# A two-layer decoder trunk: head groups of the attention in turns, sample taps of the convolution as one product and a sum, the first norm reordered

## The chip, the cores and the metric

The kernel runs on one core of a Trainium2 chip. The metric is the device time of one execution in microseconds, median of three runs. Names of engines as the profile has them: PE is TensorE (matrix products, PEld its loads of weights), DVE is VectorE, ACT is ScalarE, POOL is GpSimd, SP is SyncE, which here only issues DMAs.

## The reference, cut to what matters

One step of a two-layer decoder runs over 512 positions of a prompt and 64 of samples (8 samples of 8 positions), which share all weights: 576 columns. Each layer is a half feed-forward step, a mixer, and another half feed-forward step, each behind an RMS norm. The mixer has three branches: a causal depthwise convolution of width 31, a gated spatial product (gMLP), and attention over a sliding window of 128 positions with 8 query heads in 2 kv groups.

```python
x = x + 0.5 * swiglu(rms_norm(x, n1), gu1, dn1)
z = rms_norm(x, nm) @ w_in      # GLU | gMLP u,v | q | k | v | three gates
xp = concat([conv_prev, a])     # per sample: 30 old rows, 8 new ones
c = depthwise_conv(xp, w_conv_dw) + b_conv_dw              # 31 taps
y_a = silu(layer_norm(c)) @ w_conv_out
y_b = (u * (w_s @ layer_norm(v) + b_s)) @ w_gmlp_out
s = einsum('qkgd,skd->kgqs', q, k) * 64 ** -0.5            # per kv group k
y_c = einsum('kgqs,skd->qkgd', softmax_with_sink(s), v) @ w_o
x = x + (sig(gA)*y_a + sig(gB)*y_b + sig(gC)*y_c) @ w_out
x = x + 0.5 * swiglu(rms_norm(x, n2), gu2, dn2)
```

The prompt's attention goes by blocks of 128 queries; a block sees the key block before it and its own, the first only its own. Each sample attends to 128 cached keys and its own 8.

## The kernel before, in words

**Layout.** Activations lie with features on the 128 partitions and the 576 columns along them. Every large product of fp32 numbers is done as three products of rounded parts (high x high, high x low, low x high), each as two matmuls of 288 columns; these are the lines L327, L330 and L333 (`mm3`), a "plain" product below. The first products of a feed-forward step are combined from seven half products (`product`, L574, called from p1 to p7, and named "pair" in the list of weights), except the first three of layer 0, which are plain (`plainly`). Weights come by SP's queue into `wr` and `wc` tiles, are rounded by ACT and their low part is made by DVE, or, for some blocks of the pairs (`by_dma`), by a DMA that POOL issues and that adds in place.

**Order.** A scheduler lists the instructions of each engine by a priority: the stream of plain products advances it, `_At` shifts an engine's instruction earlier (HI, 10 million) or later (LOW). PE takes its list in order; `cpe` is PE at HI, but behind the last matmul of the stream that stands in `mark`. The mixer's small work (attention, norms, spatial products) runs as generators in `chains`: after every four input tiles of a plain product (24 matmuls, one "step") each chain is moved on by one `yield`. The numbers W_A, W_B, W_G, W_C and their like say how many steps a chain waits at a place. PSUM has two `z` tiles for the stream, two `m` tiles for norms and spatial products, and two `n` tiles, which the attention uses.

**Attention** (`attention`). After the norms and the rotation of q and k, `sample_scores` makes for each kv group 2 x (4 products of 32 columns of the array, one of 128), `sample_values` transposes the softmax and multiplies with the values. Then `scores(c, kv)` goes through 4 blocks of 2 groups one by one: four products of 256 columns in two n tiles, each read by DVE (mask added) into `sp`, then `soft`; `values(c, kv)` transposes `sp` by way of an n tile into `ptp`, and multiplies with `vT`. A kv group takes 64 rows of the array in the scores and 64 columns in the values. Two groups are in flight, and every group takes three steps.

**Convolution.** For each of four channel tiles, `tap(k)` multiplies a shifted window of `cb` with tap k and adds to `c`: one DVE instruction over the 512 prompt columns and one over the 64 sample columns, 31 times. They are put into `later` and issued in small numbers by `filler` behind products; what is left is issued ahead of the convolution's norm.

**Norms.** `square` sums the squares of x in tiles of tag g (two buffers). `rstd_steps` multiplies these sums with `ones` (L86 with `m`), takes the inverse root by Newton steps on DVE (`newton`, tiles nv, nt, no), splits the result into `oh` and spreads it over the columns by products with `idr`, the identity. `layer_norm` does the same for the gMLP and the convolution after its mean. At the start `ones` and `idr` are written after the first loads.

Of the kernel before, what the change touches and what calls it, by code (L numbers as in the profile page):

```python
# [93 lines left out]

@with_exitstack
def trunk(ctx: ExitStack, tc: tile.TileContext, a):
# [3 lines left out]
    ve, se, ge, sy = (_At(tc, e, HI) for e in (nc.vector, nc.scalar, nc.gpsimd, nc.sync))  # L100
    pe = nc.tensor
# [4 lines left out]
    lve = _At(tc, nc.vector, LOW)  # L106
# [309 lines left out]
    def square(k):  # L416
        sq = slot("g", "sq")
# [100 lines left out]
    nc.scalar.dma_start(out=vec[:, 0, 0:8], in_=a["vec"][:, 0, 0:8])  # L518
    for k in range(KD):
# [12 lines left out]
    nc.vector.tensor_copy(out=idr, in_=idn[:, 0:P])  # L532
# [4 lines left out]
    nc.vector.memset(ones, 1.0)  # L537
# [30 lines left out]
    def product(out, form, b, first):  # L568

        h, lo, n = form  # L570
        for k in range(n):
            bh, bl = b[k]
            for i, (w, r) in enumerate(((h, bh), (h, bl), (lo, bh))):
                e = pe.matmul(out=out, lhsT=w[:, k, :], rhs=r, start=first and k == 0 and i == 0,  # L574
                              stop=k == n - 1 and i == 2, skip_group_check=True)
        mark["mm"] = e.ins

    def ffn(l, f, nxt):
# [3 lines left out]
        for k0, k1 in chunks(l, f):  # L582
# [57 lines left out]
            def plainly(j):  # L640

                nonlocal r, tops
                if j == 0:
# [8 lines left out]
                    g = rstd_steps(acc["t"], 1.0 / D, EPS, r, w=1)  # L652
# [102 lines left out]
    def mixer(l, xd, nxt):  # L755
# [18 lines left out]
        def attention():  # L774
# [80 lines left out]

            def sample_scores():
                for kv in range(2):
                    zz = mtile("n")
                    r = slice(64 * kv, 64 * kv + 64)
                    for g in range(2):  # L860
                        for b in range(4):
                            cpe.matmul(out=zz[32 * b:32 * b + 32, 192 * g:192 * g + P],
                                       lhsT=qs[r, 4 * g + b].rearrange("p j t -> p (j t)"),
                                       rhs=ck[r, P * (4 * g + b):P * (4 * g + b + 1)], start=True, stop=True)
                        cpe.matmul(out=zz[:, 192 * g + P:192 * (g + 1)],
                                   lhsT=qs[r, 4 * g:4 * g + 4].rearrange("p b j t -> p (b j t)"),
                                   rhs=kk[r, TP:T], start=True, stop=True)
                    ave.scalar_tensor_tensor(out=s[:, 384 * kv:384 * (kv + 1)], in0=zz[:, 0:384], scalar=0.125,
# [4 lines left out]
            def sample_values():  # L873
# [11 lines left out]
                for kv in range(2):  # L885
                    r = slice(64 * kv, 64 * kv + 64)
                    for g in range(2):
# [3 lines left out]
                        for b in range(4):  # L891
                            bb = 4 * g + b
# [6 lines left out]
            def scores(c, kv):  # L899
# [3 lines left out]
                r = slice(64 * kv, 64 * kv + 64)  # L903
                s4 = big("sp", "sp").rearrange("p (j n) -> p j n", j=4)[:, :, 0:w]
                msk = con[:, C_MP + o0:C_MP + 256].rearrange("p (o n) -> p o n", o=1).to_broadcast([P, 2, w])
                for j in (0, 2):
                    z = mtile("n").rearrange("p (i n) -> p i n", i=2)
                    for i in range(2):
                        cpe.matmul(out=z[:, i, 0:w], lhsT=q4[r, j + i, c * P:(c + 1) * P], rhs=kk[r, k0:k0 + w], start=True, stop=True)
                    ave.scalar_tensor_tensor(out=s4[:, j:j + 2, :], in0=z[:, :, 0:w], scalar=0.125, in1=msk, op0=ALU.mult, op1=ALU.add)  # L910
                soft(s4, vcol(l, V_SP + 4 * kv, 4), lambda t: t, w, "p")
                return values(c, kv, s4, w // P, k0, r)

            def values(c, kv, s4, nk, k0, r):
                pt = big("pt", "ptp")
                for b in range(nk):
                    zt = mtile("n")
                    for j in range(4):
                        cpe.transpose(zt[:, j * P:(j + 1) * P], s4[:, j, b * P:(b + 1) * P], ident)
                    ase.activation(out=pt[:, 512 * b:512 * (b + 1)], in_=zt, func=AF.Copy)  # L920
# [9 lines left out]
            yield  # L930
            ready = [sample_values()]
            for c in range(4):
                for kv in range(2):
# [7 lines left out]
            drain(ready.pop(0))  # L941
            yield
            next(ready[0])
            yield from wait(W_B)
            drain(ready[0])
# [333 lines left out]
```

## Time and profile before

| | us |
|---|---|
| median of 3 runs (2607.34 to 2609.54) | 2608.89 |
| profiled execution | 2607.47 |
| its span in the trace | 2605.7 |
| PE busy (mean granted clock 0.995) | 2577.6 |
| DVE busy | 1910.9 |
| ACT busy | 1272.8 |
| POOL busy | 291.3 |

Busy time is that of the one profiled execution. PE's records of matmuls overlap, so that the distance from one start to the next is the cost of one, not its length. An fp32 product appears as two records: the `x8` of a group of four such products are eight records. A wait of an engine is listed with what released it; a "granted clock" of 0.5 in a stretch is the lower of TensorE's two clocks.

### The profile page before, as it was taken

How to read it: one execution, taken by the hardware profiler on the slowest of the kernel's cores; microseconds unless marked ns; L12 is line 12 of the kernel's file. 1: busy time of each engine (PE TensorE's matmuls, PEld its weight loads, DVE VectorE, ACT ScalarE, POOL GpSimd, SP SyncE). 2: the span in 40 equal slices, each digit the busy share in tenths (PEclk: the TensorE clock that was granted, in tenths of full speed). 3: DMA queues.
4: the chain of work that ended last, by engine and by line, in shares of the span. 5: the costliest groups of instructions: out<-in, count | busy, mean ns of one | idle time of the engine just before them, and what ended most of it. 6: DMA issues, size and time to landing. Idle time of an engine off the chain costs nothing.

```text
span 2605.7 us, 49108 instructions
## 1 busy us (share of the span) xinstructions
PE 2577.6 (99%) x18996; PEld 2519.0 (97%) x18996; DVE 1910.9 (73%) x3488; ACT 1272.8 (49%) x2415; POOL 291.3 (11%) x317
## 2 busy tenths in 40 slices
PE   8999999999999999999999999999999999999999
PEld 7999999988899999999999999999889999999999
DVE  7676675698897785766885766747988977766665
ACT  6455453335524564554674644533454245644543
POOL 0111010010010010111110111100200100111110
PEclk9999999999999999999999999999999999999999
DMA  5565554231222464655554655633312234655653
GB/s 179 131 147 139 125 125 132 84 87 65 66 82 81 138 150 126 147 132 132 139 129 125 146 136 132 133 116 87 85 59 68 86 96 136 145 131 143 130 143 89
DMA packets 196222, 307.48 MB, mean 118 GB/s; under 512 B 39690, under 2 KB 56970, under 8 KB 195988
## 3 DMA queue, kind: packets, MB, share of 16 engines
q1 hardware_dynamic: 159124, 237.47, 30.0%
q0 software_dynamic: 36720, 66.86, 16.0%
q8 instruction: 149, 2.44, 0.4%
q14 instruction: 85, 0.70, 0.1%
q10 hardware_dynamic: 144, 0.00, 0.0%
HBM read 292.47 MB, written 8.84 MB: 116 GB/s over the span
## 4 chain that ended last, share of the span: by engine, by line
PE 94%; DVE 3%; DMA 1%; ACT 1%; issue 1%; POOL 0%; SPq 0%; DVEq 0%; POOLq 0%; ACTq 0%
PE z L327 18%; PE z L330 17%; PE z L333 17%; PE z L574 15%; PE n L574 10%; PE m L574 10%; PE n L86 4%; PE m L86 2%; DVE w L88 1%; ACT w L88 0%; DVE x L88 0%; DMA rt<-q 0%; DMA wr<-w_gu 0%; DVE c L88 0%; DVE sums L88 0%
## 5 line engine op out<-in xcount | busy, mean ns | idle before, releaser
L88 ACT ACTIVATE w<-wr 128x512 fp32r<-128x512 f32 (+2 forms) x575 | 337.8, 604 | 625.7 <-PE z L333 487.7
L574 PE MATMUL z<-xh,w 128*128 128x288 f32 x2040 | 444.5, 299 | 1.1 <-DVE no L88 1.1
L88 ACT ACTIVATE w<-wc 128x512 fp32r<-128x512 f32 (+2 forms) x467 | 257.8, 583 | 303.2 <-PE z L333 133.1
L88 POOL DMA_DIRECT2D w<-w_gu x255 | 220.2, 864 | 1507.3 <-ACT w L88 980.7
L327 PE MATMUL z<-xh,w 128*128 128x288 f32 x1520 | 337.1, 303 | 8.0 <-ACT w L88 6.6
L88 DVE TENSOR_TENSOR w<-sums,w 128x512 fp32r<-128x512 f32 x340 | 234.4, 689 | 149.4 <-ACT w L88 145.0
L574 PEld LDWEIGHTS z<-xh,w 128*128 128x128 f32 x2040 | 338.6, 188 | 4.3 <-DVE z L88 1.3
L330 PE MATMUL z<-xl,w 128*128 128x288 f32 x1520 | 327.3, 296 | 0.0
L333 PE MATMUL z<-xh,w 128*128 128x288 f32 x1520 | 327.2, 296 | 0.0
L327 PE MATMUL z<-ah,w 128*128 128x288 f32 x1408 | 303.3, 296 | 0.4
L330 PE MATMUL z<-al,w 128*128 128x288 f32 x1408 | 301.8, 296 | 0.4 <-DVE al L88 0.2
L574 PE MATMUL z<-xl,w 128*128 128x288 f32 x1020 | 301.7, 296 | 0.0
L88 DVE TENSOR_TENSOR w<-wr,w 128x512 fp32r<-128x512 f32 (+2 forms) x373 | 240.6, 645 | 82.6 <-ACT w L88 81.6
L333 PE MATMUL z<-ah,w 128*128 128x288 f32 x1408 | 300.9, 295 | 0.0
L88 ACT ACTIVATE w<-sums 128x512 fp32r<-128x512 f32 x340 | 212.0, 624 | 139.7 <-PE z L574 73.4
L327 PEld LDWEIGHTS z<-xh,w 128*128 128x128 f32 x1520 | 245.5, 191 | 22.2 <-issue 11.7
L330 PEld LDWEIGHTS z<-xl,w 128*128 128x128 f32 x1520 | 247.5, 190 | 0.7 <-issue 0.7
L333 PEld LDWEIGHTS z<-xh,w 128*128 128x128 f32 x1520 | 246.1, 190 | 0.4 <-issue 0.3
L88 DVE SCALAR_TENSOR_TENSOR c<-cb,vec,c 128x512 f32<-128x512 f32 x480 | 244.5, 556 | 0.2
L327 PEld LDWEIGHTS z<-ah,w 128*128 128x128 f32 x1408 | 226.5, 188 | 2.5 <-DVE x L88 2.3
L330 PEld LDWEIGHTS z<-al,w 128*128 128x128 f32 x1408 | 226.5, 189 | 1.4 <-DVE al L88 1.1
L333 PEld LDWEIGHTS z<-ah,w 128*128 128x128 f32 x1408 | 226.5, 188 | 0.0
(255 smaller groups left out, 4805.0 us busy)
## 6 DMA issues: line engine op xcount, KB each, us to landing
w<-w_gu POOLq DMA_DIRECT2D x255, 256.0 KB, 4.6
wc<-w_gu SPq DMA_DIRECT2D x219, 256.0 KB, 3.0
wr<-w_in SPq DMA_DIRECT2D x184, 256.0 KB, 2.8
wr<-w_gu SPq DMA_DIRECT2D x149, 256.0 KB, 3.0
wc<-w_dn SPq DMA_DIRECT2D x75, 256.0 KB, 3.1
wr<-w_dn SPq DMA_DIRECT2D x53, 256.0 KB, 3.1
wr<-w_out SPq DMA_DIRECT2D x32, 256.0 KB, 3.2
wc<-w_dn SPq DMA_DIRECT2D x40, 128.0 KB, 2.9
```

The source lines that it names most:

```text
L86: r = f(*args, **kw)
L88: r = f(*args, **kw)
L327: pe.matmul(out=z[c], lhsT=wh, rhs=rh[:, s], start=first, stop=False)
L330: pe.matmul(out=z[c], lhsT=wh, rhs=rl[:, s], start=False, stop=False)
L333: e = pe.matmul(out=z[c], lhsT=wl, rhs=rh[:, s], start=False, stop=last)
L574: e = pe.matmul(out=out, lhsT=w[:, k, :], rhs=r, start=first and k == 0 and i == 0, stop=k == n - 1 and i == 2, skip_group_check=True)
```

## The change

1. **Attention by blocks.** `scores(c)` and `values(c)` take both kv groups, with the kv loop innermost: products of kv 0 and kv 1 stand in turns, each group with its own n tile in the scores and both in one n tile in the values, and the softmax of both is issued together. There are 4 turns of 5 steps (W_A is 4 where it was 1, W_B is 1) in place of 8 of 3. `sample_scores` and `sample_values` are turned in the same way; the `sample_scores` have their 128-column products at their end.
2. **gMLP norm.** W_G[2], the steps between the Newton steps and the products with `idr`, is 5 instead of 3.
3. **Sample taps.** The 64-column half of `tap` goes. For each channel tile four `taps(i)` are added at the end of its entries in `later` (35 instead of 31 entries): over two samples one product of an overlapping view of `cb` (2 x 8 x 31 elements, 496 columns) with the 31 taps, one sum over the last axis, and an ACT instruction that adds the bias.
4. **Start.** 22 products of `ones` with `ones` into an m tile stand ahead of the stream; `ones`, `idn` (now on ACT's DMA queue) and `idr` are written first. The squares use tag s (12 buffers), the first norm's Newton steps go to DVE and ACT at twice HI, and its sums of squares are issued ahead of the n tile's product (`next(g)`); `rms` too uses twice HI.
5. **`product`** is issued behind the last matmul in `mark`, as `cpe` is.

```diff
-W_M, W_A = 2, 1
-W_G, W_C = (4, 4, 3, 3), (2, 3, 2)
+W_M, W_A = 2, 4
+W_G, W_C = (4, 4, 5, 3), (2, 3, 2)
...
+N_WARM = 22
...
+    hve, hse = (_At(tc, e, 2 * HI) for e in (nc.vector, nc.scalar))
...
-        drain(rstd_steps(acc["t"], 1.0 / D, EPS, r))
+        drain(rstd_steps(acc["t"], 1.0 / D, EPS, r, hve, hse))
...
+    idn = slot("c", "idn")
+    nc.scalar.dma_start(out=idn[:, 0:P], in_=a["idn"])
+    hve.memset(ones, 1.0)
+    zw = mtile()
+    for i in range(N_WARM):
+        pe.matmul(out=zw[:, 0:P], lhsT=ones, rhs=ones, start=True, stop=True)
+    hve.tensor_copy(out=idr, in_=idn[:, 0:P])
...
     for k in range(KD):
-        square(k)
-    idn, selr = slot("c", "idn"), big("pt", "selr")
-    nc.sync.dma_start(out=idn[:, 0:P], in_=a["idn"])
+        square(k, "s")
...
-        for k in range(n):
+        with tc.issue_after(mark["mm"]):
+            for k in range(n):
...
-                    g = rstd_steps(acc["t"], 1.0 / D, EPS, r, w=1)
+                    g = rstd_steps(acc["t"], 1.0 / D, EPS, r, hve, hse, 1)
+                    next(g)
...
-                    for i in range(2):
-                        cpe.matmul(out=z[:, i, 0:w], lhsT=q4[r, j + i, c * P:(c + 1) * P], rhs=kk[r, k0:k0 + w], start=True, stop=True)
+                    for i in range(2):
+                        for kv, r in enumerate(KV):
+                            cpe.matmul(out=z[kv][:, i, 0:w], lhsT=q4[r, j + i, c * P:(c + 1) * P], rhs=kk[r, k0:k0 + w],
+                                       start=True, stop=True)
...
                 for b in range(nk):
-                    cpe.matmul(out=zo[r, :], lhsT=vT[:, k0 // P + b, r], rhs=pt[:, 512 * b:512 * (b + 1)],
-                               start=(b == 0), stop=(b == nk - 1))
-                ase.activation(out=q4[r, :, c * P:(c + 1) * P], in_=zo[r, :].rearrange("p (j n) -> p j n", j=4), func=AF.Copy)
+                    for kv, r in enumerate(KV):
+                        cpe.matmul(out=zo[r, :], lhsT=vT[:, k0 // P + b, r], rhs=pt[kv][:, 512 * b:512 * (b + 1)],
+                                   start=(b == 0), stop=(b == nk - 1), skip_group_check=True)
+                ase.activation(out=q4[:, :, c * P:(c + 1) * P], in_=zo.rearrange("p (j n) -> p j n", j=4), func=AF.Copy)
...
-            yield
-            ready = [sample_values()]
+            yield from wait(W_A)
+            last = sample_values()
+            next(last)
+            yield from wait(W_B)
             for c in range(4):
-                for kv in range(2):
-                    ready.append(scores(c, kv))
-                    yield from wait(W_A)
-                    if len(ready) > 2:
-                        drain(ready.pop(0))
-                    yield
-                    next(ready[-2])
-                    yield from wait(W_B)
...
+                g = scores(c)
+                yield from wait(W_A)
+                drain(last)
+                last = g
+                next(last)
+                yield from wait(W_B)
+            drain(last)
...
-                    lve.scalar_tensor_tensor(out=cs, in0=q, scalar=w[:, k:k + 1], in1=cs, op0=ALU.mult, op1=ALU.add)
+            def taps(i, cs=cs, cb=cb, w=w, b=vcol(l, V_CB + j)):
...
+                lve.tensor_tensor(out=y, in0=x0, in1=wk, op=ALU.mult)
+                lve.tensor_reduce(out=cs[:, 2 * i:2 * i + 2, :], in_=y, axis=mybir.AxisListType.X, op=ALU.add)
+                lse.activation(out=cs[:, 2 * i:2 * i + 2, :], in_=cs[:, 2 * i:2 * i + 2, :], func=AF.Identity, bias=b)
```

**What moves on PE: scores.** In the order of before, PE in layer 0 at the scores of block 1, kv 0 (z, xh and xl are the stream, n the scores; those of kv 1 stand 43 rows further on):

```order
L327 MATMUL z_6756<-xh3_75,w_6551 128x288 x2
L330 MATMUL z_6756<-xl3_83,w_6551 128x288 x2
L333 MATMUL z_6756<-xh3_75,w_6551 128x288 x2
L86 MATMUL n_6787<-kk_5051,q4_5050 128x256 x2
L86 MATMUL n_6791<-kk_5051,q4_5050 128x256 x2
L327 MATMUL z_6756<-xh4_76,w_6636 128x288 x2
```

After, PE at the same block with both groups (n_6885 and n_6893 are kv 0's two n tiles, n_6886 and n_6894 kv 1's; m are spatial products):

```order
L344 MATMUL z_6788<-xh7_79,w_6700 128x288 x2
L88 MATMUL n_6885<-kk_5074,q4_5073 128x256
L88 MATMUL n_6886<-kk_5074,q4_5073 128x256
L88 MATMUL n_6885<-kk_5074,q4_5073 128x256
L88 MATMUL n_6886<-kk_5074,q4_5073 128x256
L88 MATMUL m_6938<-ws_6738,vt_6741 128x256 x4
L88 MATMUL n_6893<-kk_5074,q4_5073 128x256 x2
L88 MATMUL n_6894<-kk_5074,q4_5073 128x256 x2
L88 MATMUL m_6938<-ws_6738,vt_6741 128x256 x2
L88 MATMUL m_6947<-ws_6738,vt_6741 128x256 x6
```

The first four products stand in turns; the second four, which need n tiles that the first still hold, stand as two of kv 0 and two of kv 1, behind four spatial products.

**What moves on PE: values.** In the order of before, PE at the values of block 1, kv 0 (those of kv 1 stand 41 rows further on, n_7365):

```order
L327 MATMUL z_7110<-xh7_79,w_7004 128x288 x2
L330 MATMUL z_7110<-xl7_87,w_7004 128x288 x2
L333 MATMUL z_7110<-xh7_79,w_7004 128x288 x2
L86 MATMUL n_7196<-ptp_7063,vT_5241 64x512 x2
L327 MATMUL z_7218<-xh0_72,w_7036 128x288 x2
L330 MATMUL z_7218<-xl0_80,w_7036 128x288 x2
```

After, PE at the values of block 1 (ptp_7153 is kv 0's, ptp_7154 kv 1's), and the first transposes of the next softmax behind them:

```order
L341 MATMUL z_7396<-xl3_83,w_7280 128x288 x2
L344 MATMUL z_7396<-xh3_75,w_7280 128x288 x2
L88 MATMUL n_7426<-ptp_7153,vT_5264 64x512
L88 MATMUL n_7426<-ptp_7154,vT_5264 64x512
L88 MATMUL n_7426<-ptp_7153,vT_5264 64x512
L88 MATMUL n_7426<-ptp_7154,vT_5264 64x512
L88 MATMUL n_7434<-idr_93,sp_7224 128x128
L338 MATMUL z_7396<-xh4_76,w_7325 128x288
L88 MATMUL n_7434<-idr_93,sp_7224 128x128
L338 MATMUL z_7396<-xh4_76,w_7325 128x288
```

Both groups' values stand in turns in one n tile; the transposes stand one by one between products of the stream.

**What moves on DVE: the first norm.** In the order of before, DVE at the start of the first norm's Newton steps (no, nt and nv):

```order
L88 TENSOR_TENSOR sums<-sums,wr 128x512
L88 TENSOR_SCALAR nv<-m 128x5
L88 TENSOR_TENSOR sums<-wc,sums 128x512
L88 TENSOR_SCALAR no<-nv 128x5
L88 TENSOR_SCALAR no<-no 128x5
L88 TENSOR_TENSOR nt<-no 128x5
L88 SCALAR_TENSOR_TENSOR nt<-nt,nv 128x5
L88 SCALAR_TENSOR_TENSOR no<-nt,no 128x5
L88 TENSOR_TENSOR nt<-no 128x5
```

After, the same steps:

```order
L90 TENSOR_SCALAR nv<-m 128x5
L90 TENSOR_TENSOR w<-wc,w 128x512
L90 TENSOR_SCALAR no<-nv 128x5
L90 TENSOR_TENSOR w<-wc,w 128x512
L90 TENSOR_SCALAR no<-no 128x5
L90 TENSOR_TENSOR w<-wc,w 128x512
L90 TENSOR_TENSOR nt<-no 128x5
L90 TENSOR_TENSOR w<-wc,w 128x512
L90 SCALAR_TENSOR_TENSOR nt<-nt,nv 128x5
L90 TENSOR_TENSOR sums<-wc,wr 128x512
L90 SCALAR_TENSOR_TENSOR no<-nt,no 128x5
L90 TENSOR_TENSOR sums<-wc,wr 128x512
```

The small steps, which stood behind one another, alternate with large ones (w and sums, parts of the next weights).

## Rows read from the trace of the kernel before

**Rows 1.** Page, part 1: busy time, share of the span, instructions.

```profile
PE 2577.6 (99%) x18996; PEld 2519.0 (97%) x18996; DVE 1910.9 (73%) x3488; ACT 1272.8 (49%) x2415; POOL 291.3 (11%) x317
```

**Rows 2.** TensorE's waits: instruction, releaser, us in total, times, longest us.

```profile
PE z L327 <- ACT w L88: 6.6, 1, 6.6
PE m L86 <- ACT oh L373: 4.2, 2, 2.5
PE m L574 <- DMA w<-w_gu: 2.1, 1, 2.1
PE m L86 <- DVE idr L532: 1.7, 1, 1.7
...
PE z L574 <- DVE no L88: 1.1, 1, 1.1
PE n L86 <- DVE ss L88: 1.0, 1, 1.0
PE n L86 <- ACT ss L88: 0.8, 1, 0.8
PE m L574 <- ACT z L88: 0.8, 2, 0.6
PE m L86 <- DVE oh L374: 0.8, 1, 0.8
```

**Rows 3.** Windows: stretch, its length, engines' busy us, PEclk, DMA share, GB/s.

```profile
534.60:541.00 6.40, 6.40 (x26) 6.22 (x27) 4.91 (x9) 2.34 (x4) 0.33 (x1) 0.51 0.41 120
59.60:63.10 3.50, 3.50 (x15) 3.50 (x16) 2.07 (x5) 0.74 (x2) 0.30 (x1) 0.51 0.91 199
1322.70:1326.10 3.40, 3.40 (x16) 3.40 (x16) 0.93 (x4) 1.07 (x2) 0.00 (x0) 0.52 0.74 213
558.00:561.40 3.40, 3.40 (x17) 3.40 (x17) 3.36 (x9) 0.69 (x1) 0.00 (x0) 0.50 0.25 84
1875.80:1879.20 3.40, 3.40 (x15) 3.28 (x16) 3.13 (x10) 1.12 (x4) 1.00 (x1) 0.54 0.47 138
...
6.60:11.60 5.00, 5.00 (x21) 5.00 (x22) 4.80 (x8) 4.87 (x9) 0.00 (x0) 1.00 1.02 381
```

**Rows 4.** Timeline of PE, sample scores: start us, length, line, operands, count.

```profile
554.61 0.42 PE L86 MATMUL n<-ck,qs 64*32 64x128 f32 x8
554.97 0.43 PE L86 MATMUL n<-kk,qs 64*128 64x64 f32 x2
```

**Rows 5.** Timeline of PE around one group of prompt scores.

```profile
593.33 0.42 PE L330 MATMUL z<-xl,w 128*128 128x288 f32 x2
593.59 0.43 PE L333 MATMUL z<-xh,w 128*128 128x288 f32 x2
593.95 1.99 PE L86 MATMUL n<-kk,q 64*128 64x256 f32 x8
595.87 0.53 PE L327 MATMUL z<-xh,w 128*128 128x288 f32 x2
```

**Rows 6.** Chain in order of time: start us, length us, engine, tile.

```profile
554.68 2.86 PE n L86 x40
...
582.25 3.76 PE n L86 x40
...
631.01 1.86 PE n L86 x4
```

**Rows 7.** DVE groups by form: operation, shapes, count, busy us, mean ns, idle.

```profile
L88 DVE TENSOR_TENSOR w<-sums,w 128x512 fp32r<-128x512 f32 x340 | 234.4, 689 | 149.4 <-ACT w L88 145.0
...
L88 DVE SCALAR_TENSOR_TENSOR c<-cb,vec,c 128x512 f32<-128x512 f32 x240 | 180.6, 752 | 0.1
...
L88 DVE SCALAR_TENSOR_TENSOR c<-cb,vec,c 128x64 f32<-128x64 f32 x240 | 86.3, 360 | 0.1
...
L88 DVE SCALAR_TENSOR_TENSOR sp<-n,con 128x512 f32<-128x512 f32 x24 | 15.9, 685 | 0.4
L88 DVE TENSOR_REDUCE m<-sp 128x4 f32<-128x1024 f32 x12 | 14.6, 1213 | 0.1
...
L88 DVE TENSOR_TENSOR nt<-no 128x5 f32<-128x5 f32 x18 | 2.9, 162 | 0.3
```

More of the change, by code (lines that the diff above doesn't have):

```diff
@@ L92, in __getattr__, with windows @@
         return call
+def windows(x):
+    dims = [list(d) for d in x.ap]
+    assert len(dims) == 4 and dims[2][0] == 0
+    dims[2][0] = dims[3][0]
+    return bass.AP(tensor=x.tensor, offset=x.offset, ap=dims)
 @with_exitstack
@@ L570, in product @@
         h, lo, n = form
-        for k in range(n):
[L572 to L575, printed above, removed]
+        with tc.issue_after(mark["mm"]):
+            for k in range(n):
+                bh, bl = b[k]
+                for i, (w, r) in enumerate(((h, bh), (h, bl), (lo, bh))):
+                    e = pe.matmul(out=out, lhsT=w[:, k, :], rhs=r, start=first and k == 0 and i == 0,
+                                  stop=k == n - 1 and i == 2, skip_group_check=True)
         mark["mm"] = e.ins
@@ L884, in sample_values @@
                 zo = mtile("n")
-                for kv in range(2):
-                    r = slice(64 * kv, 64 * kv + 64)
-                    for g in range(2):
+                for g in range(2):
+                    for kv, r in enumerate(KV):
                         i = 2 * kv + g
@@ L890, in sample_values @@
                                    start=True, stop=False, skip_group_check=True)
-                        for b in range(4):
-                            bb = 4 * g + b
+                    for b in range(4):
+                        for kv, r in enumerate(KV):
+                            i, bb = 2 * kv + g, 4 * g + b
                             cpe.matmul(out=zo[r, 32 * bb:32 * bb + 32], lhsT=cv[:, P * bb + 64 * kv:P * bb + 64 * kv + 64],
@@ L908, in scores @@
                     for i in range(2):
-                        cpe.matmul(out=z[:, i, 0:w], lhsT=q4[r, j + i, c * P:(c + 1) * P], rhs=kk[r, k0:k0 + w], start=True, stop=True)
[L910 to L920, printed above, removed]
+                        for kv, r in enumerate(KV):
+                            cpe.matmul(out=z[kv][:, i, 0:w], lhsT=q4[r, j + i, c * P:(c + 1) * P], rhs=kk[r, k0:k0 + w],
+                                       start=True, stop=True)
@@ new lines, in scores, with values @@
+                    for kv in range(2):
+                        ave.scalar_tensor_tensor(out=s4[kv][:, j:j + 2, :], in0=z[kv][:, :, 0:w], scalar=0.125, in1=msk,
+                                                 op0=ALU.mult, op1=ALU.add)
+                for kv in range(2):
+                    soft(s4[kv], vcol(l, V_SP + 4 * kv, 4), lambda t: t, w, "p")
+                return values(c, s4, w // P, k0)
+            def values(c, s4, nk, k0):
+                pt = [big("pt", "ptp") for kv in range(2)]
+                for kv in range(2):
+                    for b in range(nk):
+                        zt = mtile("n")
+                        for j in range(4):
+                            cpe.transpose(zt[:, j * P:(j + 1) * P], s4[kv][:, j, b * P:(b + 1) * P], ident)
+                        ase.activation(out=pt[kv][:, 512 * b:512 * (b + 1)], in_=zt, func=AF.Copy)
@@ L1054, in tap @@
                                              op0=ALU.mult, op1=ALU.add)
-                    lve.scalar_tensor_tensor(out=cs, in0=q, scalar=w[:, k:k + 1], in1=cs, op0=ALU.mult, op1=ALU.add)
+            def taps(i, cs=cs, cb=cb, w=w, b=vcol(l, V_CB + j)):
+                o = ST + TP + 2 * i * (ST + NS)
+                y = slot("s", "taps")[:, 0:2 * NS * CW].rearrange("p (n s k) -> p n s k", n=2, s=NS)
+                x0 = cb[:, o:o + 2 * (ST + NS)].rearrange("p (n o s) -> p n o s", n=2, o=1)
+                x0 = x0[:, :, :, 0:CW].to_broadcast([P, 2, NS, CW])
+                x0 = windows(x0)
+                wk = w.rearrange("p (n s k) -> p n s k", n=1, s=1).to_broadcast([P, 2, NS, CW])
+                lve.tensor_tensor(out=y, in0=x0, in1=wk, op=ALU.mult)
+                lve.tensor_reduce(out=cs[:, 2 * i:2 * i + 2, :], in_=y, axis=mybir.AxisListType.X, op=ALU.add)
+                lse.activation(out=cs[:, 2 * i:2 * i + 2, :], in_=cs[:, 2 * i:2 * i + 2, :], func=AF.Identity, bias=b)
             for k in range(CW):
                 later.append(lambda k=k, tap=tap: tap(k))
+            for i in range(NB // 2):
+                later.append(lambda i=i, taps=taps: taps(i))
         def gate(tag, name, fill):
```

44 lines of the change are left out of this document (19 added, 25 removed).

## The prediction, made before the changed kernel ran

> **What bounds the kernel now.** I read the page first: its busy table and its chain of waits say that TensorE sets the time, busy 2577.6 of 2605.7 us [rows 1]. A busy TensorE says little about what it could save, so I went on to the list of TensorE's own waits [rows 2], to its granted clock [rows 3], and to the pitch (start to start) of its matmuls in the timeline. Two plain matmuls start every 0.26 us, 0.13 us each [rows 5]. The waits are short and few: 6.6 us before the first matmul, the longest group after it 4.2 us. But some are followed by a stretch at half clock: 6.4 us at a granted 0.51 after the layer norm's wait, 3.5 us after a wait for a transfer, 3.4 us three more times [rows 3]. [...] So the time falls only if TensorE's matmuls get shorter, or if waits with their slow stretches go.
>
> **Attention: pairs of head groups.** Each of the two kv head groups uses half of the array: 64 rows in the score products, 64 columns in the products with the values. Before, the groups run one after the other, with other work between. The change lets kv 0 and kv 1 alternate.
> Does a second half run beside the first? The sample scores show it for columns: eight records (four products in four column strips of 32) start 0.36 us before the next tile [rows 4]. A score record of 256 columns costs 1.92/8 = 0.24 us [rows 5], so one of 128 costs about 0.12 and eight in a row 0.96. So strips overlap fully. For rows no trace of before has a pair side by side; bounds are nothing and a half, and I take the half, since the strips are the nearest rows.
> *Values:* a block with two key blocks costs 1.86 us per head group [rows 6], with about 0.1 us of entry; three such blocks of two groups, and one with half the work (1.1 with its entry), are 6 x 1.95 + 2 x 1.1 = 13.9 us a layer. Alternating, the order has all of them in pairs: 7.0. Saved 6.9 a layer, **-13.8**.
> *Scores:* eight records of 256 columns take 1.92 us [rows 5], 2.0 with the entry, six times a layer, and half that twice: 14 us. Here the order matters. Only the first four products of blocks 0, 1 and 2 alternate; the second four stand as two of kv 0, then two of kv 1, and block 3 is cut in four such pieces. They need an n tile of PSUM that the first four still hold (two buffers), and the scheduler took them as it expected the buffers. So of 14 us only the alternating fours halve: 0.45 + 2 x 0.9 = 2.2 a layer, **-4.4** (ends 0 and -8).
> *Sample part:* scores 2.9 us, values 3.8 [rows 6], 6.7 a layer. All alternate, so I halve them: 3.4 a layer, **-6.8** (ends -3 and -8).
>
> **Layer norm and start of the sample part.** The gMLP norm's matrices (oh) come two steps later after their Newton chain: some 120 plain matmuls instead of 73, 6 us more. That covers the wait for ACT's oh, 4.2 us over both layers [rows 2], and with it the half-clock stretch of 6.4 us, which costs half, 3.2 [rows 3]; with a second piece at the same place (0.8) **-8.2** (ends 0 and -8.2). The wait of 1.0 us for the sample scores and its twin for ACT go too, since W_A is 4: **-1.8**.
>
> **Products in the order of the code.** `product` now stays behind the last matmul of the stream. Before, a first-half product was pulled ahead at the first pairs and waited 2.1 us for its transfer [rows 2], then 3.5 us ran at 0.51 [rows 3]: 2.1 + 1.7 = 3.8. It now stands some 60 matmuls, 8 us, later: **-3.8** (ends -3.8 and +1). At the start of layer 1, waits of 0.8 for ACT's z and 1.1 for DVE's no [rows 2] lie around 3.4 us at 0.52 [rows 3], worth 1.7; the new order puts 12 plain matmuls ahead of the product that waited, but the sums of squares come earlier and may wait about 1: **-2.6** (ends -3.6 and +2). The two other half-clock stretches follow the sample scores and the sample values [rows 3], 1.7 us each; those stretches become shorter, I take one of two: **-1.7** (ends 0 and -3.4).
>
> **The start.** 22 products of `ones` run on TensorE while it would wait for data (6.6 us) [rows 2]. [...] Against it: the first norm's sums stand before the n tile (48 matmuls, 6.3 us), but in DVE's order the 13 small steps (0.16 us) now alternate with eleven large ones (0.69) [rows 7]: 9.7 us, so TensorE waits 3.4 where it waited 1.7 for idr [rows 2]. Together **+1** (ends -2 and +4).
>
> **Sample taps.** A sample tap costs 0.36 us, 240 of them 86 us; the 512-wide tap of 0.752 us stays [rows 7]. Sixteen products and sums over taps of 496 elements, at 0.69 each, from the 512-wide subtraction, are 22 us: VectorE is 64 us freer. TensorE is the bound, so this counts **0** by itself; its cover is that nobody on TensorE waits for a tap until the conv norm. There the queue of taps is 16 entries a layer longer, which the fillers no longer empty, and the conv norm starts 52 matmuls (7 us) later, with 74 instead of 96 matmuls to hide its last third: with the last gMLP product, now drained early, **+3** (ends 0 and 6).
>
> **What the denser attention costs.** Four blocks in 20 steps instead of eight groups in 24 put the softmax closer. Between the scores of blocks 2 and 3 DVE has 24.5 us by its order (4 x 0.685, 2 x 1.213 [rows 7], 22 of about 0.75 or 0.69, ten small ones), and TensorE 125 plain matmuls (16.5) + values 2.0 + scores 3.1 + 16 transposes priced as plain matmuls 2.1 = 23.7; between blocks 1 and 2 the same sums are 29 against 26. So DVE falls behind by about 4 us a layer, and TensorE feels it where it waits for an n tile, since each second score product waits for a read of 0.685 behind what is queued. 4 us a layer: **+8** (ends 3 and 20).
>
> **Sum.** -13.8 - 4.4 - 6.8 - 8.2 - 1.8 - 3.8 - 2.6 - 1.7 + 1 + 3 + 8 = -31.1. The profiled execution took 2607.5 us, 1.8 more than its span and 1.4 less than the median of 2608.9: 2576.4 on its own scale, **2578** on the median's.
>
> **Rivals.**
> (1) *Evacuation becomes the limit.* The four n tiles of a block pass through two buffers, so every pair waits for DVE or ACT behind their queues; the freed TensorE time is given back. At the upper end of that term (20 instead of 8) 2590. For it: DVE's sums above exceed TensorE's. Against: ACT has room, and 64 us of DVE work are gone. [...]
> (2) *Rows do not overlap, or nothing does.* Without row pairs 4.4 + about 3 of the sample part are missing: 2585; without column pairs too, all 25: 2603. Against it: the strips of rows 4.
> (3) *Better.* No new waits (-11): 2567; with the other half-clock stretch gone too and the start and layer-1 terms at their good ends, 2561.
> (4) *Slower: each change of the array's half drains it.* The order alternates some 80 times a layer. Entry into a small-tile group costs about 0.1 us and its exit 0.2 (595.87 - 593.95 is 0.2 over eight records of 0.216) [rows 5]. If each alternation paid 0.25 and nothing overlapped, 160 x 0.25 = 40 us come on top of 2603: 2643. It decides from 0.07 us an alternation on (11 us over 160). Against it: four strips started within one 0.36 us [rows 4].
> The order itself shows that the pairs do alternate, so "it does not do what it says" holds only for the second score fours, and is in the sum.
>
> **How the numbers follow.** Forecast 2578 (2568 to 2586): 0.48. Better (2556 to 2568): 0.17. Evacuation (2586 to 2600): 0.20. No row or no overlap (2583 to 2604): 0.09. Slower: 0.06. A measurement of this kernel tells about 0.2%, 5 us, from no change. Below 2603.7 lie all but the last case and a part of the fourth: faster 0.91, same 0.03, slower 0.06. The range 2558 to 2600 leaves out the slow case, the outer parts of rival 3 and of rival 2.
>
> **What would show it.** Value records of one block starting in pairs, two within 0.45 us: the values term. Second score fours at the old pitch. No wait for oh in the gMLP norms and no half clock behind. No wait for w_gu in the first pairs. New TensorE waits on n tiles behind DVE: their total against my 8. A first norm's wait of 3 to 4 us. Wrong if alternating records keep the old pitch, or if new waits on n tiles pass 20 us.

## The result: 90 us slower

The changed kernel took 2699.4 us (median of four runs, 2695.32 to 2703.93) against 2608.89 (2607.34 to 2609.54): a ratio of 1.0348, 95% interval 1.033 to 1.0366. The forecast was 2578 with a range of 2558 to 2600.

On its page TensorE does the same amount of work as before [rows 1], 2573.2 us, but in a span of 2697.9, and the chain of waits, 94% TensorE's and 3% VectorE's before, is now 14% VectorE's (part 1 of the page, and part 4, the chain by engine):

```profile
PE 2573.2 (95%) x19040; PEld 2514.2 (93%) x19040; DVE 1910.2 (71%) x3304; ACT 1279.8 (47%) x2439; POOL 297.7 (11%) x317
...
PE 80%; DVE 14%; issue 2%; ACT 2%; DMA 1%; POOL 0%; SPq 0%; DVEq 0%; ACTq 0%; POOLq 0%
```

The chain by engine of before:

```profile
PE 94%; DVE 3%; DMA 1%; ACT 1%; issue 1%; POOL 0%; SPq 0%; DVEq 0%; POOLq 0%; ACTq 0%
```

TensorE's list of waits (instruction, releaser, us in total, times, longest) has two entries at its head that before's list does not have [rows 2]:

```profile
PE z L591 <- DVE z L90: 67.0, 53, 1.3
PE z L591 <- ACT p L90: 32.2, 16, 7.1
PE m L88 <- DVE sg L1034: 3.9, 2, 2.3
PE z L591 <- DVE g L90: 3.2, 1, 3.2
PE m L88 <- DVE lns L750: 3.0, 2, 1.5
PE n L88 <- DVE qs L90: 2.8, 2, 1.7
...
PE n L88 <- DVE sp L90: 0.6, 2, 0.3
```

L591 is `product`, the half products of the feed-forward steps. Where the time went is seen when the span is cut at the first matmul of each stage: start and first feed-forward step, mixer of layer 0, the two steps between the mixers, mixer of layer 1, last step. The windows of after (stretch, its length, busy us of the engines, granted clock, DMA share, GB/s):

```profile
0.00:437.40 437.40, 410.79 (x3004) 405.31 (x3005) 291.08 (x505) 223.31 (x406) 50.03 (x65) 0.98 0.56 137
437.40:929.40 492.00, 486.10 (x3634) 468.29 (x3633) 394.51 (x681) 212.66 (x434) 40.03 (x28) 1.00 0.30 90
929.40:1778.40 849.00, 794.44 (x5851) 782.53 (x5850) 564.54 (x977) 431.20 (x796) 112.70 (x134) 0.99 0.55 127
1778.40:2271.00 492.60, 484.56 (x3635) 466.69 (x3634) 393.78 (x681) 212.76 (x434) 39.80 (x28) 1.00 0.30 89
2271.00:2697.90 426.90, 397.34 (x2926) 391.35 (x2924) 266.26 (x462) 199.86 (x371) 55.11 (x64) 0.99 0.52 121
```

and two windows of before, the mixer of layer 0 and the two steps behind it:

```profile
414.60:917.80 503.20, 499.88 (x3635) 476.81 (x3634) 399.10 (x773) 212.64 (x422) 34.28 (x27) 0.99 0.29 88
917.80:1707.50 789.70, 785.82 (x5850) 779.68 (x5849) 560.09 (x977) 427.81 (x797) 112.70 (x134) 1.00 0.58 136
```

| stage (us) | before | after | after, with products free (below) |
|---|---|---|---|
| start and first feed-forward step | 414.6 | 437.4 | 411.2 |
| mixer, layer 0 | 503.2 | 492.0 | 491.9 |
| two feed-forward steps | 789.7 | 849.0 | 785.8 |
| mixer, layer 1 | 501.3 | 492.6 | 493.3 |
| last feed-forward step | 396.9 | 426.9 | 395.9 |
| span | 2605.7 | 2697.9 | 2578.1 |

Both mixers became shorter, by 11.2 and 8.7 us, which is the part of the change that the prediction spent most of its words on. The feed-forward steps, in which the attention has no part, became 22.8 + 59.3 + 30.0 = 112 us longer. In the two steps of the middle window TensorE is idle 849.0 - 794.4 = 54.6 us; in before's it was 3.9.

**One such wait, close up.** A pair of a feed-forward step is made by seven half products, p1 to p7; p6 adds into an m or n tile, p2 into the first half of a z tile. The timeline of TensorE (start, length, line, operation, count, idle before) at one of the 53:

```profile
135.13 0.29 PE L591 MATMUL m<-fh,w 128*128 128x288 f32 x1
136.69 0.40 PE L591 MATMUL z<-xh,w 128*128 128x288 f32 x1 [1.26 <-DVE z L90]
```

and VectorE at the same time:

```profile
134.24 0.75 DVE L90 SCALAR_TENSOR_TENSOR t<-t,g 128x576 f32<-128x576 f32 x1
134.91 0.69 DVE L90 TENSOR_TENSOR w<-sums,w 128x512 fp32r<-128x512 f32 x1
135.51 0.75 DVE L90 TENSOR_TENSOR u<-u,t 128x576 f32<-128x576 f32 x1
136.18 0.46 DVE L90 TENSOR_TENSOR z<-m,p 128x288 f32<-128x288 f32 x1
```

The last matmul of p6 (into the m tile) starts at 135.13. VectorE's sum of it (z<-m,p, 0.46 us) stands in its queue behind elementwise operations of 0.7 us, two of which are left when that matmul starts, and is done at 136.64. The next product, p2, is listed behind the sum and waits for it: its first matmul starts at 136.69, 1.56 us after the one ahead of it where the pitch is 0.13. So a wait that the list prices at 1.26 us costs 1.43.

The same place in before, TensorE and then VectorE:

```profile
131.10 0.29 PE L574 MATMUL m<-fh,w 128*128 128x288 f32 x1
131.24 0.30 PE L574 MATMUL z<-xh,w 128*128 128x288 f32 x1
...
132.57 0.30 PE L574 MATMUL z<-xl,w 128*128 128x288 f32 x1
132.70 0.36 PE L574 MATMUL z<-xh,w 128*128 128x288 f32 x1
```

```profile
131.48 0.75 DVE L88 TENSOR_TENSOR u<-u,t 128x576 f32<-128x576 f32 x1
132.15 0.46 DVE L88 TENSOR_TENSOR z<-m,p 128x288 f32<-128x288 f32 x1
```

VectorE is no faster there: the sum starts 1.05 us after p6's last matmul, as it does after (136.18 - 135.13). But p2 is not next on TensorE. The eleven matmuls from 131.24 to 132.57 belong, by the order of the code, to p5, a product of the next pair; the scheduler had put them between, and p2 starts at 132.70, when the sum is done, at the usual pitch. After, `product` may not pass the last matmul of the stream, so p5 stands behind p2 and covers nothing.

**The account.** 67.0 + 32.2 + 3.2 us of waits in the feed-forward steps, 69 times some 0.16 that the list doesn't count (11), and longer stretches at half clock at the start of the steps (next fence: 25 us busy at a mean of about 0.54, so some 11.5 lost), less the waits that before had there (5.7 in its list, the largest of them in rows 2) and its two half-clock stretches (3.4) [rows 2, 3]: 116 us, where 112 + 1.6 (the start became shorter by that) = 114 were measured.

The granted clock of after in the stretches around the five longest waits of the half products, and in one with four waits of 1.26 us (second row):

```profile
57.10:68.90 11.80, 8.16 (x35) 7.85 (x36) 7.25 (x14) 4.67 (x10) 0.86 (x1) 0.57 0.31 73
125.00:175.00 50.00, 44.94 (x333) 44.00 (x332) 36.46 (x62) 30.71 (x57) 10.42 (x13) 1.00 0.64 137
934.60:941.90 7.30, 5.36 (x22) 5.37 (x23) 4.04 (x8) 3.03 (x7) 1.51 (x2) 0.54 0.48 107
1358.30:1368.70 10.40, 5.75 (x24) 5.75 (x25) 7.81 (x14) 3.90 (x8) 0.86 (x1) 0.51 0.40 97
2276.20:2283.80 7.60, 5.87 (x26) 5.87 (x27) 3.84 (x7) 2.83 (x6) 1.54 (x2) 0.55 0.44 97
```

### The profile page after: what moved, and what is told of

The parts are those of the page before. It is cut to its first block, busy times and chain, and to the rows that moved or that the text cites. A ratio compares the mean times of both kernels' runs of the same rounds, so it can differ in the third digit from the quotient of the medians.

```text
span 2697.9 us, 49040 instructions
## 1 busy us (share of the span) xinstructions
PE 2573.2 (95%) x19040; PEld 2514.2 (93%) x19040; DVE 1910.2 (71%) x3304; ACT 1279.8 (47%) x2439; POOL 297.7 (11%) x317
## 4 chain that ended last, share of the span: by engine, by line
PE 80%; DVE 14%; issue 2%; ACT 2%; DMA 1%; POOL 0%; SPq 0%; DVEq 0%; ACTq 0%; POOLq 0%
PE z L591 16%; PE z L338 15%; PE z L344 14%; PE z L341 14%; PE n L591 9%; PE m L591 8%; DVE w L90 3%; DVE c L90 2%; PE n L88 2%; DVE u L90 2%; DVE t L90 2%; PE m L88 1%; DVE z L90 1%; ACT w L90 1%; DMA rt<-q 1%
## 5 line engine op out<-in xcount | busy, mean ns | idle before, releaser
L591 PE MATMUL z<-xh,w 128*128 128x288 f32 x2040 | 455.3, 303 | 102.3 <-DVE z L90 67.0
L591 PEld LDWEIGHTS z<-xh,w 128*128 128x128 f32 x2040 | 342.6, 190 | 120.3 <-DVE z L90 79.5
L591 PE MATMUL z<-xl,w 128*128 128x288 f32 x1020 | 303.5, 298 | 0.0
L90 DVE SCALAR_TENSOR_TENSOR c<-cb,vec,c 128x512 f32<-128x512 f32 x240 | 198.5, 827 | 3.3
```

The costliest lines, as they stand in the source:

```text
L90: r = f(*args, **kw)
```

## Experiments

All ratios are to the kernel before, timed on the same chip as the variant. Its median was 2603.8, 2609.0 and 2607.7 us on the three chips, so variants from different chips are compared by their ratios.

### Products free again

```diff
-        with tc.issue_after(mark["mm"]):
-            for k in range(n):
+        for k in range(n):
...
```

> The changed kernel, with `product` as it was before (no longer held behind the last matmul of the stream). Theory A (strict order): holding the products took away the cover of the waits for DVE's sum (53 times, 67 us) and ACT's copy (16 times, 32 us) in the feed-forward phases, which grew by 22.8 + 59.3 + 30.0 = 112 us, while the two mixers got 20 us shorter. So these phases come back: about 2609 - 20 = 2589 us (2580 to 2595), and the list of TensorE's waits no longer has the 53 waits of z for DVE's z. Rival B (DVE and ACT are late in these phases because of other parts of the change, the squares in another tag or the norm's steps at twice HI): the waits stay, over 2650 us.

Measured 2581.99 us, ratio 0.9913 (0.9898 to 0.9928): 23 us faster than before and, by the two ratios, 113 faster than the changed kernel. TensorE's list begins with the mixers' waits, and no half product waits for a sum for more than 0.3 us:

```profile
PE m L88 <- DVE sg L1033: 4.6, 2, 2.3
```

Rival B falls; the stages are in the table above. This one wrapper is the whole loss.

### The same edit alone, on the kernel before

```diff
-        for k in range(n):
+        with tc.issue_after(mark["mm"]):
+            for k in range(n):
...
```

> The kernel before, with that one edit of `product` alone. Theory A: the feed-forward phases grow as in the changed kernel, about 2609 + 110 = 2719 us (2705 to 2730), with some 53 waits of z for DVE's z of 1.3 us each. Rival B: 2600 to 2615 us, no such waits.

Measured 2713.97 us, ratio 1.0423 (1.0406 to 1.0439), 110 us slower. The waits are those of the changed kernel to 0.1 us, with the old attention, taps and start:

```profile
PE z L575 <- DVE z L88: 66.9, 53, 1.3
PE z L575 <- ACT p L88: 32.2, 16, 7.1
```

### Products held, the sum written behind p2

```diff
                 product(o["c"], weights(o["what"], 3), fac["b"][3], False)
-                ve.tensor_tensor(out=o["z"][:, 1, h1], in0=o["c"], in1=o["p5"], op=ALU.add)
...
                     p6(o)
                     p2(o)
+                    add6(o)
```

(`add6` is the same sum as a function of its own.)

> The changed kernel, products still held, but DVE's sum into the second half of z is written in the code behind the next product (p2, which writes the first half of the same z tile) instead of ahead of it. Theory A1 (p2 waits only because the sum is listed ahead of it on the same tile, not because it needs the sum's result): the 53 waits of 1.27 us go, 67 us, about 2632 us (2622 to 2645), the 16 waits for ACT's copy stay. Rival A2 (DVE is simply 1.3 us late in each pair, and the next product that reads the sum or its inputs waits in p2's place): over 2680 us.

Measured 2614.97 us, ratio 1.0038 (1.0025 to 1.005). The 53 waits are gone and nothing took their place, so p2 did not need the sum's result: it writes the first half of z, the sum the second, and waits only because the sum was written ahead of it on the same tile. The gain, 81 us by the ratios, is more than the 67 of the list; the 53 x 0.16 that the list leaves out are 8 of the difference, and the 5 or 6 that are left lie within the noise of the two ratios. ACT's copies stay:

```profile
PE z L591 <- ACT p L90: 32.1, 16, 7.1
```

### Products held, sum and copy written behind p2

The pairs of a feed-forward step are worked off in four chunks. In the first pair of each chunk, `save(o)` (ACT copies the second half of z) moves behind p2 too.

```diff
                     p5(o)
                     seed(o)
-                    save(o)
...
                     p2(o)
+                    save(o)
                     p6(o)
+                    add6(o)
```

> The changed kernel, products still held; besides DVE's sum behind p2 (as in the variant before it, 2615 us), in the first pair of each chunk ACT's copy of the second half of z (save) is written behind p2 too. Theory A (the whole loss is products waiting for a sum and a copy that stand ahead of them on the same z tile): the 16 waits for ACT's p, 32 us, go; 2585 us (2578 to 2595), level with the free products. Rival C (holding the products costs by itself, since PE then has nothing else to take at each wait): 2605 to 2618 us.

Measured 2598.38 us, ratio 0.9961 (0.995 to 0.9973), between the two forecasts. The waits for p are gone, but p2 in a first pair adds to what ACT's seed puts there, a wait that is real, 0.48 us in most chunks:

```profile
PE z L591 <- ACT z L90: 10.9, 16, 2.0
...
PE z L591 <- DVE g L90: 3.2, 1, 3.2
...
PE z L591 <- ACT xh L90: 1.1, 1, 1.1
PE z L591 <- DVE xl L90: 1.0, 1, 1.0
```

These four are 16 us, where the free products have 5 at the same places; the difference is 11, and by the ratios this kernel is 12.5 behind them. So a strict order costs no more than the waits that it leaves uncovered; theory A holds, but for the real dependency that it had left out.

### Attention alone

The kernel before with the new blocks, sample part and W_A = 4 (the body of `attention` as in the change).

```diff
-W_M, W_A = 2, 1
+W_M, W_A = 2, 4
...
-            def scores(c, kv):
+            def scores(c):
```

> The kernel before, with the attention part alone (blocks with both kv groups, sample part, W_A 4). Theory T (neighbours on the two halves run beside each other): values 13.2 us, score fours 4.3, sample scores and values 2 x (2.86 - 1.27) + 2 x (3.76 - 1.98) = 6.7, waits for ss 1.8, in all 26, less new waits of some 6 us: 20 us faster than before (14 to 26). Rival N (the mixers' gain in the variant with free products came from the norm's waits and the taps): less than 8 us faster.

Measured 2589.32 us, ratio 0.9919 (0.9905 to 0.9934): 21 us faster. Here the n tiles do wait for VectorE, four times:

```profile
PE n L86 <- DVE sp L88: 8.3, 4, 3.8
```

In the changed kernel that entry is 0.6 us, and 4.8 with free products and the old taps (below), so the new taps take off some 4 of it.

### Turns taken away, blocks kept

Free products; within each block the kv loop stands outside, so kv 1's products follow kv 0's.

```diff
...
-                for b in range(nk):
-                    for kv, r in enumerate(KV):
+                for kv, r in enumerate(KV):
+                    for b in range(nk):
...
```

> As the changed kernel with `product` as before, but within each block the kv loop is put outside again, so that the products of kv 0 and kv 1 stand one group behind the other (the blocks, steps and everything else stay). Theory T (products on the two halves of the array run beside each other when they stand in turns): by the trace of the changed kernel eight records of the values take 1.87 us for both groups (1.86 for one group before), so 6 x 1.86 us here; the alternating score fours 1.06 instead of 1.92, 4 us in all; the sample part some 4: 15 to 24 us slower than the variant with turns. Rival S (the mixers became shorter by other means, fewer waits and n tiles, and turns give nothing): within 4 us of it.

Measured 2587.43 us, ratio 0.9934 (0.9919 to 0.9949), 5 us behind the variant with turns, where 15 to 24 were expected. The two mixers' stretch up to the gMLP's products is 254.9 and 254.5 us here, 253.5 and 254.4 with turns, so the attention itself has about 1.5 of the 5; the rest lies in the feed-forward steps (789.9 to 785.8), which the edit doesn't touch. The values show why. TensorE's timeline at the values of one group alone, before (4 records, and the plain matmul behind):

```profile
630.94 1.93 PE L86 MATMUL n<-ptp,vT 128*64 128x512 f32 x4
632.80 0.53 PE L327 MATMUL z<-xh,w 128*128 128x288 f32 x2
```

both groups in turns, in the changed kernel (8 records, and the transpose behind):

```profile
664.36 1.94 PE L88 MATMUL n<-ptp,vT 128*64 128x512 f32 x8
666.23 0.33 PE L88 MATMUL n<-idr,sp 128*128 128x128 f32 x1
```

and both without turns, two products of kv 0 and then two of kv 1:

```profile
642.18 1.94 PE L88 MATMUL n<-ptp,vT 128*64 128x512 f32 x8
644.05 0.33 PE L88 MATMUL n<-idr,sp 128*128 128x128 f32 x1
```

They take 1.86, 1.87 and 1.87 us. Eight records in the time of four needed no turns here: it was enough that the other half's products stood right behind. The first four score products of block 1 show the same for halves by rows: without turns they take 1.07 us, with turns 1.06 (their fence stands in the part on the prediction).

```profile
598.11 1.14 PE L88 MATMUL n<-kk,q 64*128 64x256 f32 x8
599.18 0.74 PE L88 MATMUL m<-ws,vt 128*128 128x256 f32 x4
```

The sample values lose 0.5 us by the edit in layer 0 (2.41 us, 1.91 with turns). Theory T was right that the halves overlap and wrong that turns bring it about.

### The norm's wait alone

```diff
-W_G, W_C = (4, 4, 3, 3), (2, 3, 2)
+W_G, W_C = (4, 4, 5, 3), (2, 3, 2)
```

> The kernel before, with W_G[2] alone 5 instead of 3. Theory P (the prediction's step): the wait for oh (4.2 us) and its half-clock stretch go, 8 us faster (5 to 9). Rival M (the wait moves to a later product of the same chain, as the 2.3 us for sg and 3.5 us at half clock behind it in each layer of the changed kernel suggest): within 3 us of before.

Measured 2600.55 us, ratio 0.9971 (0.9955 to 0.9987): 8 us faster (3 to 12). The wait for oh has left the list; what came is a wait for qs, ahead of the sample scores, so rival M's mechanism is there too:

```profile
PE z L327 <- ACT w L88: 6.7, 1, 6.7
PE n L86 <- DVE qs L88: 3.4, 2, 1.8
```

Behind the first of these waits TensorE runs at a granted 0.50 from 549.5 to 556.2 us, 6.7 us, about as long as the stretch that went (6.4 [rows 3]). In the two traces the mixers' stretch up to the gMLP's products is 3.4 and 1.4 us shorter (263.0 and 262.9 against 266.4 and 264.3), so 4.8 of the 8 us are found there.

### The start alone

The kernel before with part 4 of the change.

```diff
+    for i in range(N_WARM):
+        pe.matmul(out=zw[:, 0:P], lhsT=ones, rhs=ones, start=True, stop=True)
...
-                    g = rstd_steps(acc["t"], 1.0 / D, EPS, r, w=1)
+                    g = rstd_steps(acc["t"], 1.0 / D, EPS, r, hve, hse, 1)
+                    next(g)
```

> The kernel before, with the start alone: 22 products of ones, identity first, squares in another tag, the norm's steps at twice HI, sums ahead of the n tile. By the variant with free products, whose pairs' first block ends 2.9 us earlier: 3 us faster (0 to 5). Prediction's step: 1 us slower (2 faster to 4 slower).

Measured 2607.59 us, ratio 0.9998 (0.9987 to 1.0008): no difference that can be measured. In its trace the first half product starts 1.6 us earlier (53.88 against 55.48), and the mixers' wait for oh is 6.0 us where before had 4.2 [rows 2], though the edit does not touch the gMLP norm.

### The taps alone

The kernel before with part 3 of the change.

```diff
-                    lve.scalar_tensor_tensor(out=cs, in0=q, scalar=w[:, k:k + 1], in1=cs, op0=ALU.mult, op1=ALU.add)
...
+            for i in range(NB // 2):
+                later.append(lambda i=i, taps=taps: taps(i))
```

> The kernel before, with the sample taps alone (16 products and sums in place of 240 small taps). Theory: VectorE is 64 us freer, TensorE is the bound, and the conv norm waits 1.5 us a layer for lns as in the changed kernel, since more taps are left over at its start: 3 us slower (0 to 5). Rival: the freer VectorE shortens other waits and it is 3 to 8 us faster.

Measured 2615.56 us, ratio 1.0021 (1.0012 to 1.0031): 5 us slower. The conv norm's wait for lns (1.5 us a layer) is there as in the changed kernel. From the first of the gMLP's products to the first of the convolution's a layer takes 163.4 us, where before took 161.0, and from there to the output's 25.8 for 25.0: 6.4 us in both layers, where 3 to 8 were lost in all. The wait for oh is 6.7 us, where before had 4.2 [rows 2]; since it is 6.0 with the start alone and the old taps, the new taps are not shown to lengthen it:

```profile
PE m L86 <- ACT oh L381: 6.7, 2, 3.8
PE m L86 <- DVE lns L740: 2.9, 2, 1.5
```

### Free products with the old taps

```diff
+                    lve.scalar_tensor_tensor(out=cs, in0=q, scalar=w[:, k:k + 1], in1=cs, op0=ALU.mult, op1=ALU.add)
...
-            for i in range(NB // 2):
-                later.append(lambda i=i, taps=taps: taps(i))
```

> Free products and the sample taps as before; attention, norm wait and start as changed. If the parts add up (attention -20, norm wait -8, start -1, taps +6.6 measured alone): 2609 - 29 = 2580 on the scale of the first runs, about 6.5 us faster than free products with the new taps, 2575 us (2571 to 2580) on the scale of their call. Rival (parts overlap: with the attention's blocks the taps' freer VectorE is needed): within 2 us of free products, 2582 us.

Measured 2584.77 us, ratio 0.9916 (0.9899 to 0.9932): level with the new taps (0.9913). The parts do not add up here. From the gMLP's products to the convolution's the old taps give 2.4 us a layer back (159.7 to 162.1), but the attention's stretch is longer by 3.2 and 3.9 (256.7 and 258.3 to 253.5 and 254.4), where VectorE is busier (197.5 and 197.1 us to 188.7 and 188.8) and n tiles wait for it. Over the whole kernel VectorE is busy for 1911.8 us with the old taps and for 1902.3 with the new, only 9.5 less. The n tiles' waits with the old taps:

```profile
PE n L88 <- DVE sp L90: 4.8, 6, 2.2
```

### The new taps in a queue of the old length

Each of the four products with sums is issued in one entry with one of the last four taps.

```diff
+            def entry(k, tap=tap, taps=taps):
+                tap(k)
+                if k >= CW - NB // 2:
+                    taps(k - CW + NB // 2)
...
-                later.append(lambda k=k, tap=tap: tap(k))
-            for i in range(NB // 2):
-                later.append(lambda i=i, taps=taps: taps(i))
+                later.append(lambda k=k, entry=entry: entry(k))
```

> Free products, taps as changed, but each of the four products with sums of a channel tile is issued in one entry with one of its last four taps, so that the queue of taps has 124 entries a layer again instead of 140. Theory Q (the taps cost 6.5 us because the longer queue leaves more for the conv norm): 6 us faster than with 140 entries, 2576 us (2572 to 2579). Rival D (the cost lies in the added instructions themselves): 2580 to 2585 us.

Measured 2580.21 us, ratio 0.9897 (0.9883 to 0.9912), the best of all, though its interval overlaps that of 140 entries. On the scale of the forecasts (0.9897 x 2603.8) it is 2577 us, in theory Q's range. The stretch from the gMLP's products to the convolution's comes back to 159.8 us with all the added instructions in it, and the wait for lns is gone, so those 2.4 us go with the queue's length; in the attention some 1.5 us a layer are lost again. The 4 us between the two are not clear of the noise.

### Two more waits moved by a step

Old taps, W_R 7, and one step more ahead of the last three products of each spatial product.

```diff
-W_V, W_S, W_N, W_T, W_R, W_B = 2, (2, 1, 1, 1, 1), 3, 2, 6, 1
+W_V, W_S, W_N, W_T, W_R, W_B = 2, (2, 1, 1, 1, 1), 3, 2, 7, 1
...
-            yield
+            yield from wait(2)
             z = mtile()
             mm(z[:, 0:P], 512, 640, 256, 384, TS)
```

> As the variant without the new taps, and two waits are moved by a step: the sample scores come one step later (W_R 7) and the last three products of each spatial product one step later. Theory: the waits for qs (3.0 us) and sg (4.6 us, with 3.5 us at half clock behind each) go: 8 to 10 us faster, 2566 us (2561 to 2570). Rival M (the waits move on to the softmax and the next spatial product): within 3 us of that variant.

Measured 2584.32 us, ratio 0.991 (0.9895 to 0.9925): level with the variant it was made from. The waits for sg and qs went, and the waits for vt (2.1 to 4.2 us) and for ss (1.9) took their place.

## Why the prediction was wrong, point by point

- **Products in the order of the code** is the step that failed. It was priced at -3.8 at the first pairs and -2.6 at the start of layer 1: the places where before had a wait and where the order showed a move. The edit holds the half products of all 85 pairs; away from the starts of the steps before's half products wait for nothing, and I took an empty list to mean that there was nothing to lose. It was empty because of what the edit takes away. Measured alone, +110 us. In the changed kernel it also did not remove the wait that it was aimed at: in place of 2.1 us for a transfer there are 3.2 for DVE's g and 1.9 for ACT's p, and at the start of layer 1 one wait of 7.1 us for ACT's p.
- No rival held it. The rival on the slow side, drained halves at 2643 with a chance of 0.06, was a mechanism of the attention; rival 1, evacuation, was looked for on the n tiles. It did not come true here: n tiles waited 0.6 us for VectorE in the changed kernel, and 4.8 and 8.3 in two variants that were faster than before all the same.
- **Attention**, -13.8, -4.4 and -6.8: right in size, and in mechanism but for one reason. Values: 1.87 us for both groups instead of one. Scores: the first fours take 1.06 us for both (from one start to the next); so halves by rows overlapped here, as the strips by columns did (eight records in 0.36 us [rows 4]). The second fours were put at the old pitch, 1.92, because they stand as two and two. They take 1.65, behind a wait of 0.32, and the order is not the reason that they take longer than the first: two and two took 1.07 above. Here, by the starts of the single records, kv 1's two begin 0.59 us after kv 0's (623.03 against 622.44) and overlap them in part. TensorE's timeline at block 1's scores:

```profile
620.32 1.13 PE L88 MATMUL n<-kk,q 64*128 64x256 f32 x8
621.38 0.74 PE L88 MATMUL m<-ws,vt 128*128 128x256 f32 x4
622.44 1.73 PE L88 MATMUL n<-kk,q 64*128 64x256 f32 x8 [0.32 <-DVE sp L90]
624.09 1.21 PE L88 MATMUL m<-ws,vt 128*128 128x256 f32 x8
```

  Sample scores and values take 1.2 and 1.9 us instead of 2.86 and 3.76 [rows 6], 7.0 less in both layers. With the waits for ss these terms are 26.8, less the 8 for the denser attention 18.8; 21 were measured alone.
- **The norm's wait**, -8.2: the number came out alone (8, with an interval of 3 to 12), the working only in part, so some of it is luck: the wait for oh and its half clock went, and waits for qs (3.4 us) with 6.7 us at half clock came. In the changed kernel waits for qs (2.8 us, 3.4 us at a granted 0.50 behind the one of 1.7) and sg (3.9 us, at full clock behind both) give part of it back; with free products the half clock stands behind sg (4.6 us, 3.4 us at 0.50 behind each).
- **Waits of the sample scores**, -1.8: wrong, 2.8 us for qs took their place. **Half-clock stretches**, -1.7: too small a term to tell.
- **Start**, +1 (ends -2 and +4): within its bounds, nothing measured. The first norm's wait, put at 3.4 us, was 0.9 and 0.2. The +1 also holds a gain from the 22 early products, of a size that no run shows; the traces show 0.27 us: in the changed kernel the stream starts at 8.67 us with its matmuls 0.13 us apart, before at 6.57 with the first 21 at 0.24 [rows 3], and its 31st matmul starts at 12.72 against 12.99.
- **Taps**, +3 (ends 0 and 6): alone 5, within its bounds, in company nothing. The 64 us that VectorE was to be freer are wrong: sixteen products and sums are one layer's. The changed kernel's trace has 32 of each, 22.0 and 20.7 us, the wide taps take 0.827 us instead of 0.752 [rows 7], and VectorE is busy for 1910.2 us where it was 1910.9 [rows 1] (with free products the new taps free 9.5). The forecast counted 0 for them, but they also stood against rival 1.
- **Denser attention**, +8 (ends 3 and 20): too much in the changed kernel (0.6 us on n tiles), right in the variant with the attention alone (8.3).
- Without the two product terms the sum was -24.7, 2584 us; the kernel with free products measures 0.9913 x 2608.9 = 2586 (2582 to 2590). That the other terms add up so well is in part luck: the 8 for n tiles did not come, and with free products waits for sg (4.6 us, with 3.4 us lost at half clock) and qs (3.0), which no term had, did. One line of the diff, costed at two places and governing 85 pairs, outweighed all of them more than four times.

## What to carry to other kernels

A rule on order must be priced at every place that it governs, above all where the engine never waits: look at what stands between a product and the read of its result, and ask whether the rule lets it stand there. In a list in which each instruction waits on whole tiles, a sum that is written one line later can save much of what a reordering saves (here 81 of 113 us). Products on the two halves of the array overlapped here once they were neighbours on TensorE (1.87 us for both groups' values, 1.86 for one [rows 6]); turns added little (1.87 us with them and without).

## What was not expected of the hardware

Four products of two halves took as long without turns as with them (1.87 us, against 1.86 for two products of one half [rows 6]). And the clock: the stretch from 125 to 175 us holds four waits of 1.26 us, 5 us idle of 50, at a granted clock of 1.00, while waits of 3.2 and 1.9 us shortly behind one another, of 3.6 and 3.8, and of 7.1 us stand in stretches with 5 to 8 us of work whose mean is 0.51 to 0.57, with a granted 0.50 for most of each. The length of one wait alone does not tell which: in the changed kernel's mixer 3.4 us at 0.50 follow a wait of 1.7 us for qs, while the stretch behind a wait of 1.6 us for sg (588 to 592 us) has 1.00. Of the 6.4 us that the new taps alone cost behind the gMLP's products 2.9 are the waits for lns; where the rest comes from no run here shows.
